# Sums of squares of the DeltaNet queries: from transposes and ScalarE squares to products with a column of ones

## The chip, the cores and the metric

The kernel runs on one NeuronCore of one Trainium2 chip. The metric is the device time of one execution in microseconds (us), as the median of several executions of the same program. Profiles are taken of one execution each. The five engines are named as in the profile: PE (TensorE matmul; PEld is its weight load), DVE (VectorE), ACT (ScalarE), POOL (GpSimd) and SP (SyncE, which issues most of the DMAs).

## The reference, cut to what matters

The kernel computes a two-layer encoder trunk over 1024 tokens of width 1024. The first (even) layer has mLSTM heads and gated DeltaNet heads that share one input projection; the second has a convolution and dilated attention. The part that the change touches is the normalisation of the DeltaNet queries, one of four heads of 128 channels at a time:

```python
def _l2n(t):
    return t * lax.rsqrt(jnp.sum(t * t, axis=-1, keepdims=True) + EPS)
...
    qkv = jax.nn.silu(_dwconv(dqkv, dn_conv_w))
    bq, bk, bv = _split(qkv, (B_HEADS * B_DK, B_HEADS * B_DK, B_HEADS * B_DV))
    q = _l2n(bq.reshape(bsz, s, B_HEADS, B_DK).astype(f32)) * (B_DK ** -0.5)
    k = _l2n(bk.reshape(bsz, s, B_HEADS, B_DK).astype(f32))
```

Each query is divided by the root of the sum of its 128 squares. The kernel leaves the queries as they are and brings the factor in at the end, on the output of the heads (`rq2` and `rqs`, from `ssq`). So for each head a number per token is needed, the sum over channels of the squared query, and it is needed only late.

## The kernel before, in words

**Layout.** Projections come out of PE as channels by tokens: 128 channels of one head on the partitions, 1024 tokens in the row, in two halves of 512 tokens. A projection (`project`, `prod`) is 24 matmuls of 128x512 for each half (three products of split operands for each of 8 blocks of the width). The halves go to two PSUM banks (`ibank`, two buffers), and a half can start only when the bank that it takes has been copied out.

**A query head, `dn_q(h)`.** ScalarE copies both halves into a page `xp` with a margin for the convolution (line 397). `conv5` makes the five taps on VectorE from `xp` into a page `y` (lines 402 and 404), then ScalarE writes the tanh into `xp` (line 405) and VectorE multiplies it back into `y` (line 406), which finishes the SiLU up to a factor of two. `y` is stored to HBM (`qT_d`, line 731). Then, for each half of the tokens, `turn` transposes four blocks of 128x128 with PE into a PSUM bank of the tag "t", and `squares` reads each block with a ScalarE Square whose accumulator gives the sum over the row (line 411): tokens stand on the partitions there, so the sum over channels is a sum along the row. Each such Square is followed by an instruction that reads the accumulator into a column of `ssq`. The key heads (`dn_k`) do the same, but need the transposed keys anyway.

**What the heads share.** Pages with the tag "b" (128x1024 float32) have three buffers, and every head takes two of them, one for `xp` and one for `y`; the mLSTM values take one each. A page is taken again when all readers of its last tile are done. The PSUM tag "t" has one buffer: the turns of keys, gate rows, queries, values and mLSTM keys and values all pass through it one after the other, and so do the products of the modulation (`ada_cols`, and `gps` in `modulation`).

**Order.** The steps are called in a fixed list: `dn_q` of head 0, `dn_v` of head 0, `m_q` 0, `dn_q` 1, `m_q` 1, then `systems`, `dn_q` 2 and 3, `m_k` 1, `m_v` 0, 2, 3, 1, `m_k` 0, and then the inversion of the DeltaNet systems, the mLSTM and the rest. From `systems` on, each half of a projection that ends issues one `dn_system` behind its last matmul on PE (`pace["sys"]`): products of keys (`KK`), decays on POOL and ScalarE, products on VectorE (line 649) and stores to `nd_d`, which the inversion reads when all eight are there. A generator, `modulation`, is stepped at each weight load and puts its loads, ScalarE scalings (line 444), POOL sums (line 446) and products between. Within these bounds a planner in the compiler orders each engine's instructions by its own simulated time and assigns the buffers; engines then run their instructions in that order.

`adaps` in the trace is a bank that holds products of the same kind as those of the change: 128 columns of weights against the column `one` (line 139 is the line of every matmul, line 158 that of every transpose).

Of the kernel before, what the change touches and what calls it, by code (L numbers as in the profile page):

```python
# [11 lines left out]
AF = mybir.ActivationFunctionType  # L12
# [5 lines left out]
P = 128  # L18
T = 1024
D = 1024  # L20
KT = 8
NCH = 8
# [34 lines left out]
def trunk(ctx, tc, x, c, norm_g, ada_w, ada_b, ev_w_in, ev_m_gate_b, ev_dn_dt_bias, ev_dn_a_log,  # L57
          ev_dn_conv_w, ev_m_norm_g, ev_dn_norm_g, ev_w_out, od_w_in, od_dw_w, od_dw_b, od_ln_g,
          od_ln_b, od_w_out, rel_bias, final_g, sel, onehot, seen, out):
    nc = tc.nc  # L60
# [40 lines left out]
    def page(name, shape=(P, T), dt=F32, tag="b"):  # L101
        return pg.tile(list(shape), dt, tag=tag, name=name, bufs=PAGES[tag])
# [3 lines left out]
    def bank(name, shape=(P, 512), tag="t"):  # L106
        return psb.tile(list(shape), F32, tag=tag, name=name, bufs=BANKS[tag])
# [19 lines left out]
    def nm(s):  # L127
        uid[0] += 1
        return f"{s}_{uid[0]}"
# [7 lines left out]
    def mm(o, l, r, s, e, shared=False):  # L137

        return nc.tensor.matmul(o, lhsT=l, rhs=r, start=s, stop=e, skip_group_check=shared).ins  # L139
# [3 lines left out]
    one = cst.tile([P, 1], F32, name="one")  # L143
# [12 lines left out]
    def tr(o, i):  # L156
        k = i.shape[0]
        nc.tensor.transpose(o, i, ident[:k, :k])  # L158
# [128 lines left out]
    def in0(c0, name, use):  # L287
        project(wsplit(w0[:, c0:c0 + P], name), hT, name, use)
# [26 lines left out]
    def columns(g):  # L315
        for tiles, b0 in zip(ada[g], (2 * g, 8 + 2 * g)):
# [5 lines left out]
                          in_=wgr.rearrange("p k (g c) -> p k g c", g=4))  # L322
# [67 lines left out]
    ssq = cst.tile([P, NCH, 4], F32, name="ssq")  # L390
    ivr = cst.tile([P, NCH, 4], F32, name="ivr")

    def conv_in():
        xp = page(nm("xp"), (P, T + 4))
        nc.gpsimd.memset(xp[:, 0:2], 0.0)
        nc.gpsimd.memset(xp[:, T + 2:T + 4], 0.0)
        return xp, lambda hf, ps: nc.scalar.copy(out=xp[:, 2 + hf * 512:514 + hf * 512], in_=ps)

    def conv5(xp, cidx, y):

        w_ = lambda j: cw[:, j * 12 + cidx:j * 12 + cidx + 1]
        nc.vector.tensor_scalar(out=y, in0=xp[:, 0:T], scalar1=w_(0), scalar2=None, op0=ALU.mult)
        for j in range(1, 5):
            nc.vector.scalar_tensor_tensor(out=y, in0=xp[:, j:j + T], scalar=w_(j), in1=y, op0=ALU.mult, op1=ALU.add)
        nc.scalar.activation(out=xp[:, 0:T], in_=y, func=AF.Tanh, scale=0.5)
        nc.vector.scalar_tensor_tensor(out=y, in0=xp[:, 0:T], scalar=1.0, in1=y, op0=ALU.add, op1=ALU.mult)

    def squares(b_, ss, q, h):
        junk = wk.tile([P, P], F32, tag="junk", name=nm("junk"))
        for i in range(4):  # L410
            nc.scalar.activation(out=junk, in_=b_[:, i * P:(i + 1) * P], func=AF.Square,
                                 accum_out=ss[:, q * 4 + i, h:h + 1])

    def turn(src, q, tag="t"):
        b_ = bank(nm("turn"), tag=tag)
        for i in range(4):
            tr(b_[:, i * P:(i + 1) * P], src[:, (q * 4 + i) * P:(q * 4 + i + 1) * P])
        return b_
# [54 lines left out]
    for h in range(2):  # L473
        xp, use = conv_in()
# [6 lines left out]
    for h in range(2, 4):  # L481
        xp, use = conv_in()
# [86 lines left out]
    for e in range(2):  # L569
        nc.sync.dma_start(out=woldb[e * 64:e * 64 + 64],  # L570
                          in_=wold_d.rearrange("(d q e) c -> e d q c", d=2, e=2)[e:e + 1].to_broadcast([64, 2, 2, NCH]))
# [6 lines left out]
    for src, dst in ((cs1, col1), (cs2, col2)):  # L578
        for q in range(2):
            b_ = turn(src, q)  # L580
            nc.vector.tensor_copy(out=dst[:, q * 4:q * 4 + 4, :].rearrange("p c (g r) -> p c g r", r=8),
                                  in_=b_.rearrange("p (c g r) -> p c g r", c=4, g=4)[:, :, :, 0:8])
# [143 lines left out]
    def dn_q(h):  # L726
        xp, use = conv_in()
        in0(1552 + h * P, "dq", use)
        y = page(nm("qT"))
        conv5(xp, h, y)  # L730
        nc.sync.dma_start(out=qT_d[h], in_=y)
        for q in range(2):
            squares(turn(y, q), ssq, q, h)

    def dn_v(h):
        xp, use = conv_in()
# [190 lines left out]
    for step, n in [(dn_q, 0), (dn_v, 0), (m_q, 0), (dn_q, 1), (m_q, 1), (systems, 0), (dn_q, 2), (dn_q, 3), (m_k, 1), (m_v, 0), (m_v, 2), (m_v, 3), (m_v, 1), (m_k, 0)] + [(dn_inverse, 0), (mlstm, 0), (dn_v, 1), (gate_chunk, 0), (dn_v, 2), (gate_chunk, 1), (dn_v, 3)]:  # L927
        step(n)
# [264 lines left out]
    for g, (a0, n) in enumerate(((0, N1), (N1, N23))):  # L1193
        for h in range(8):
            nc.sync.dma_start(out=z_d[g, h].rearrange("(q l) -> q l", l=513)[:, 0:n],
                              in_=nb_d[h:h + 1, a0:a0 + n].to_broadcast([P, n]))
# [411 lines left out]
```

## Time and profile before

| | |
|---|---|
| median of 3 runs | 1437.38 us (1429.26 to 1439.33) |
| the profiled execution | 1441.71 us, its span 1439.9 us |
| granted PE clock, mean of the span | 0.951 |
| PE busy | 1319.2 us (92%), 7299 instructions |
| DVE busy | 881.4 us (61%) |
| ACT busy | 589.2 us (41%), 1411 instructions |
| POOL busy | 471.8 us (33%) |
| largest shares of the chain that ended last | PE 59%, DVE 15%, DMA 15%, ACT 4% |

The span is the time from the first to the last instruction of the profiled execution. Busy time is the sum over an engine's instructions, where overlapping ones count once. PE's clock has two levels, 1.2 and 2.4 GHz; a granted clock of 0.50 is the lower one throughout and 1.00 the upper one. The chain that ended last is followed back from the last instruction, at each step to what released it.

### The profile page before, as it was taken

What the parts mean: (1) busy time and instruction counts of PE and PEld (TensorE: products, weight loads), DVE (VectorE), ACT (ScalarE), POOL (GpSimd) and SP (SyncE); (2) the same over time, 40 slices, a digit from 0 to 9 for tenths busy, and PEclk for the clock granted to TensorE, in tenths of its full rate; (3) what the DMA queues carried; (4) which work ended last, traced back from release to release, by engine and by line L of the source; (5) the groups of instructions that cost most, each with busy time, mean ns of one, the idle gap of its engine ahead of it and who ended that gap; (6) DMA issues with size and microseconds to landing.
All of it is one profiled execution on the core that took longest, in us unless ns stands there. A gap on an engine that the chain in (4) does not pass through costs nothing.

```text
span 1439.9 us, 20401 instructions
## 1 busy us (share of the span) xinstructions
PE 1319.2 (92%) x7299; PEld 1049.9 (73%) x7299; DVE 881.4 (61%) x1622; ACT 589.2 (41%) x1411; POOL 471.8 (33%) x357
## 2 busy tenths in 40 slices
PE   3887989988989999999999978999999999998998
PEld 2776767866777777888788757767777777776776
DVE  6779647169445332558654469997895553436444
ACT  5354575444645225544543211132326634335222
POOL 3455546443534412103340124211243232123120
PEclk9898889999999999899999989999999999998999
DMA  9433446746997786656651632111241153335412
GB/s 311 133 88 112 120 132 199 170 121 183 320 210 224 238 234 190 187 155 196 210 187 42 152 81 59 45 30 41 91 124 32 54 175 95 108 122 182 125 62 103
DMA packets 232985, 203.02 MB, mean 141 GB/s; under 512 B 59360, under 2 KB 191092, under 8 KB 232756
## 3 DMA queue, kind: packets, MB, share of 16 engines
q1 hardware_dynamic: 212083, 191.23, 45.1%
q10 hardware_dynamic: 20800, 10.49, 2.5%
q8 instruction: 58, 0.95, 0.3%
q14 instruction: 44, 0.35, 0.1%
HBM read 148.45 MB, written 56.88 MB: 143 GB/s over the span
## 4 chain that ended last, share of the span: by engine, by line
PE 59%; DVE 15%; DMA 15%; ACT 4%; SPq 3%; issue 3%; POOL 2%; POOLq 0%; ACTq 0%; DVEq 0%
PE y L139 12%; PE z L139 8%; PE sc L139 4%; DVE u L1247 4%; PE ob L139 3%; PE gb L139 3%; PE dq L139 2%; PE av L139 2%; PE pT L158 2%; PE ak L139 2%; PE mo L139 2%; PE mq L139 2%; PE aq L139 2%; PE ga L139 2%; DVE U L212 1%
## 5 line engine op out<-in xcount | busy, mean ns | idle before, releaser
L265 POOL TENSOR_TENSOR wlo<-wraw,whi 128x1024 fp32r<-128x1024 f32 x60 | 162.0, 2702 | 344.3 <-ACT whi L264 344.3
L1247 DVE SCALAR_TENSOR_TENSOR u<-xp,U,u 128x1009 f32<-128x1009 f32 (+14 forms) x120 | 175.0, 1491 | 1.0
L264 ACT CAST whi<-wraw 128x1024 fp32r<-128x1024 f32 x60 | 62.7, 1046 | 131.0 <-PE gb L139 46.3
L446 POOL TENSOR_TENSOR U<-U 128x512 f32<-128x512 f32 x56 | 81.9, 1463 | 75.7 <-ACT U L444 74.8
L139 PE MATMUL z<-hhi,wlo 128*128 128x512 f32 x256 | 104.5, 408 | 0.0
L139 PE MATMUL z<-hhi,whi 128*128 128x512 f32 x256 | 104.2, 407 | 0.0
L139 PE MATMUL z<-hlo,whi 128*128 128x512 f32 x256 | 103.9, 406 | 0.0
L139 PE MATMUL y<-wohi,mhi 128*128 128x512 f32 x240 | 97.4, 407 | 2.6 <-ACT mhi L1056 2.1
L139 PE MATMUL y<-wolo,mhi 128*128 128x512 f32 x240 | 96.5, 402 | 0.2 <-POOL wolo L1048 0.2
L139 PE MATMUL y<-wohi,mlo 128*128 128x512 f32 x240 | 95.9, 401 | 0.1
L444 ACT ACTIVATE U<-U,cs 128x512 f32<-128x512 f32 x64 | 46.1, 723 | 66.6 <-DMA U<-in_ada_w_dram 64.2
L1399 DVE COPY U<-pT 128x512 f32<-128x512 f32 x48 | 32.5, 688 | 52.7 <-PE pT L158 52.5
L602 POOL TENSOR_SCALAR_AFFINE_SELECT E<-E 128x512 f32<-128x512 f32 x32 | 23.7, 743 | 107.4 <-DMA E<-gc_d 59.0
L139 PEld LDWEIGHTS z<-hlo,whi 128*128 128x128 f32 x256 | 48.7, 190 | 12.3 <-issue 2.0
L139 PEld LDWEIGHTS z<-hhi,wlo 128*128 128x128 f32 x256 | 48.7, 190 | 11.5 <-issue 0.8
L139 PEld LDWEIGHTS z<-hhi,whi 128*128 128x128 f32 x256 | 48.8, 190 | 11.3 <-issue 0.7
L139 PEld LDWEIGHTS y<-wohi,mhi 128*128 128x128 f32 x240 | 45.8, 192 | 13.4 <-ACT mhi L1056 2.5
L139 PEld LDWEIGHTS y<-wohi,mlo 128*128 128x128 f32 x240 | 45.6, 190 | 11.5 <-DVE mlo L1057 0.9
L139 PEld LDWEIGHTS y<-wolo,mhi 128*128 128x128 f32 x240 | 46.0, 192 | 10.7 <-POOL wolo L1048 0.4
L1376 ACT ACTIVATE pt<-pt,o 128x256 f32<-128x256 f32 (+1 forms) x64 | 31.3, 489 | 53.3 <-DVE o L1372 45.4
L1372 DVE CUSTOM_DVE_ANT_0 pt<-sc,U 128x256 f32<-128x256 f32 (+1 forms) x64 | 25.8, 403 | 40.0 <-PE sc L139 20.6
L139 PE MATMUL sc<-ak,aq 128*128 128x256 f32 (+1 forms) x128 | 44.4, 428 | 6.4 <-DVE o L1374 5.4
(453 smaller groups left out, 3584.6 us busy)
## 6 DMA issues: line engine op xcount, KB each, us to landing
wraw<-in_ev_w_in_dram SPq DMA_DIRECT2D x32, 512.0 KB
U<-in_ada_w_dram SPq DMA_DIRECT2D x64, 256.0 KB
wraw<-in_od_w_in_dram ACTq DMA_DIRECT2D x20, 512.0 KB
x<-in_x_dram SPq DMA_DIRECT2D x11, 512.0 KB
ada<-in_ada_w_dram SPq DMA_DIRECT2D x10, 512.0 KB
od_d<-o SPq DMA_DIRECT2D x64, 66.0 KB
U<-od_d SPq DMA_DIRECT2D x4, 1056.0 KB
U<-gc_d SPq DMA_DIRECT2D x8, 512.0 KB
```

The source lines that it names most:

```text
L139: return nc.tensor.matmul(o, lhsT=l, rhs=r, start=s, stop=e, skip_group_check=shared).ins
L158: nc.tensor.transpose(o, i, ident[:k, :k])
L212: nc.vector.scalar_tensor_tensor(out=acc, in0=w_, scalar=cs[:, k:k + 1], in1=acc, op0=ALU.mult, op1=ALU.add)
L264: nc.scalar.copy(out=hi, in_=raw)
L265: nc.gpsimd.tensor_tensor(out=lo, in0=raw, in1=f(hi), op=ALU.subtract)
L444: nc.scalar.mul(out=t_ if k else acc, in_=t_, mul=cs[:, k:k + 1])
L446: nc.gpsimd.tensor_tensor(out=acc, in0=acc, in1=t_, op=ALU.add)
L602: nc.gpsimd.affine_select(out=ap, in_=ap, pattern=[[0, 4], [pat, P]], compare_op=ALU.is_ge, fill=NEG, base=0, channel_multiplier=cm_)
L1247: nc.vector.scalar_tensor_tensor(out=y[:, lo:hi], in0=xp[:, lo + d:hi + d], scalar=w_, in1=y[:, lo:hi], op0=ALU.mult, op1=ALU.add)
L1372: nc.vector.tensor_tensor_reduce(out=x1_, in0=ps[:, c0:c1], in1=bias[:, e, c0:c1], scale=1.0, scalar=1e30, op0=ALU.add, op1=ALU.min, accum ...
L1376: nc.scalar.activation(out=x1_, in_=x1_, func=AF.Exp, scale=-1.0, bias=mn1, accum_out=o2[:, 0, 128 + e:129 + e])
L1399: nc.vector.tensor_copy(out=PT, in_=tb)
```

## The change

For each of the four query heads, ScalarE squares the whole of `y` once, as channels by tokens, into the page `xp`. Eight products then take a block of 128 channels by 128 tokens of the squares as weights and the column of ones as the moving operand: each gives the sums over channels of 128 tokens as one column, tokens on the partitions, in one bank of the tag "t". VectorE copies the eight columns to `ssq`. The eight transposes of the head, its eight ScalarE squares by token and the eight reads of the accumulator go. `y` is then read last by the Square and the store, and `xp` by the products.

```diff
@@ -729,8 +729,12 @@
         y = page(nm("qT"))
         conv5(xp, h, y)
         nc.sync.dma_start(out=qT_d[h], in_=y)
-        for q in range(2):
-            squares(turn(y, q), ssq, q, h)
+
+        nc.scalar.activation(out=xp[:, 0:T], in_=y, func=AF.Square)
+        ps = bank(nm("sq"), (P, NCH))
+        for ch in range(NCH):
+            mm(ps[:, ch:ch + 1], xp[:, ch * P:(ch + 1) * P], one, True, True)
+        nc.vector.tensor_copy(out=ssq[:, :, h:h + 1], in_=ps.rearrange("p (c o) -> p c o", o=1))
```

## Rows read from the trace of the kernel before

**Rows 1.** The page, busy time: us, share of the span, instructions.

```profile
PE 1319.2 (92%) x7299; PEld 1049.9 (73%) x7299; DVE 881.4 (61%) x1622; ACT 589.2 (41%) x1411; POOL 471.8 (33%) x357
```

**Rows 2.** Busy by stretch: stretch, us, engines' busy us, granted clock, DMA share, GB/s.

```profile
195.00:235.00 40.00, 31.89 (x129) 23.80 (x128) 27.32 (x48) 24.23 (x76) 22.25 (x18) 0.79 0.67 190
```

**Rows 3.** Timeline of PE, 199 to 231 us: start, us, instruction [idle before <-releaser].

```profile
199.91 0.60 PE L158 MATMUL turn<-ident,qT 128*128 128x128 f32 x4
202.17 0.66 PE L158 MATMUL turn<-ident,qT 128*128 128x128 f32 x4 [1.21 <-ACT junk L411]
204.48 1.86 PE L139 MATMUL gps<-U,one 128*1 128x512 f32 x2 [1.66 <-ACT junk L411]
...
210.80 0.79 PE L139 MATMUL dq<-hhi,whi 128*128 128x512 f32 x1 [0.68 <-ACT xp L397]
...
228.25 1.12 PE L158 MATMUL turn<-ident,qT 128*128 128x128 f32 x4 [2.08 <-ACT junk L411]
230.29 0.79 PE L139 MATMUL mk<-hhi,whi 128*128 128x512 f32 x1 [0.93 <-ACT xp L397]
```

**Rows 4.** Instructions of `junk`: ns min/median/max, first and last start.

```profile
L411 ACT ACTIVATE junk<-turn x64: 244/277/300, 114.8 to 269.2; 128x128 f32<-128x128 f32 x64
L411 ACT ACTIVATION_READ_ACCUMULATOR junk<-turn x64: 185/194/229, 115.0 to 269.3; 128x1 f32 x64
...
L229 ACT ACTIVATE junk<-x x8: 1044/1057/1064, 4.3 to 38.1; 128x1024 f32<-128x1024 f32 x8
```

**Rows 5.** Instructions of `turn`, those on the queries.

```profile
L158 PE MATMUL turn<-ident,qT x32: 270/272/476, 199.9 to 267.7; 128*128 128x128 f32 x32
```

**Rows 6.** Instructions of `adaps`.

```profile
L139 PE MATMUL adaps<-one,U x64: 164/250/373, 13.5 to 418.1; 128*128 128x1 f32 x64
L220 DVE TENSOR_TENSOR modc<-adaps,vec x12: 140/151/162, 14.8 to 418.3; 128x2 f32<-128x2 f32 x8, 128x4 f32<-128x4 f32 x4
```

**Rows 7.** Timeline of PE around four products with the column of ones.

```profile
273.38 0.40 PE L139 MATMUL mv<-hhi,whi 128*128 128x512 f32 x1
273.62 0.95 PE L139 MATMUL adaps<-one,U 128*128 128x1 f32 x8
274.43 0.48 PE L139 MATMUL mv<-hlo,whi 128*128 128x512 f32 x1
274.75 0.40 PE L139 MATMUL mv<-hhi,wlo 128*128 128x512 f32 x1
```

**Rows 8.** Chain that ended last, in order of time: start, us, what.

```profile
148.31 7.78 PE mq L139 x23
...
164.21 7.04 PE dq L139 x30
...
200.07 0.44 PE turn L158 x4
...
203.44 4.64 DMA nd_d<-U
```

**Rows 9.** Timeline of DVE: last step of query head 0, value head 0, query head 1.

```profile
157.71 1.21 DVE L406 SCALAR_TENSOR_TENSOR qT<-xp,qT 128x1024 f32<-128x1024 f32 x1
159.02 0.75 DVE L402 TENSOR_SCALAR vT<-xp,cw 128x1024 f32<-128x1024 f32 x1
...
166.75 1.23 DVE L406 SCALAR_TENSOR_TENSOR vT<-xp,vT 128x1024 f32<-128x1024 f32 x1 [1.19 <-ACT xp L405]
...
217.87 1.23 DVE L406 SCALAR_TENSOR_TENSOR qT<-xp,qT 128x1024 f32<-128x1024 f32 x1 [5.62 <-ACT xp L405]
```

**Rows 10.** Timeline of ACT: copies of query heads 1 and 3 into their pages.

```profile
168.53 0.60 ACT L397 COPY xp<-dq 128x512 f32<-128x512 f32 x1
...
229.66 1.06 ACT L397 COPY xp<-dq 128x512 f32<-128x512 f32 x2
```

**Rows 11.** Timeline of SP: the store of query head 0.

```profile
162.33 0.55 SPq L731 DMA_DIRECT2D qT_d<-qT  x1
```

**Rows 12.** Timeline of PE: the first matmul behind the projection of query head 1.

```profile
174.33 0.39 PE L139 MATMUL mq<-hhi,whi 128*128 128x512 f32 x1
```

## The prediction

> **What bounds the kernel now.** I read the page's busy times first: PE is busy 92% of the span, no other engine over 61% [rows 1]. So a change pays where it takes away PE's idle time, its time at the low clock, or work on PE; time taken from ScalarE alone is hidden. Then I read busy time by stretch, where the query heads run. The stretch of 195 to 235 us is the poor one: PE is busy 31.89 of 40 us, so idle for 8.1, at a mean granted clock of 0.79 [rows 2]. The timeline of PE names the reason. The two turns of query head 0 stand one behind the other, since the one bank "t" must first be emptied by four ScalarE squares: 1.21 us of idle before the second turn, 1.66 before the next user of the bank. Head 1 has the same at 228.25, with 2.08 us [rows 3]. And twice PE starts a projection late, at 210.80 and 230.29, because ScalarE had not copied the last one out [rows 3]; that copy waited for a page "b", and the pages were held by tiles whose turns stood in the queue for the bank. So here bank "t" and the three pages set the pace together, and the change touches both: it shortens the stay in the bank and changes which page of a head is held to the end.
>
> **The change part by part.**
>
> *ScalarE.* 32 squares of 0.277 us and as many reads of 0.194 go, 15.1 us if none overlapped. Four squares of 128x1024 come, at 1.06 us each by the row of the same function on the same shape, 4.2 us [rows 4]. Some 11 us less for an engine at 41% [rows 1]: alone worth nothing, since PE hides it.
>
> *PE's work.* The 32 transposes that go [rows 5] cost 0.44 us for four [rows 8], 3.5 us in all. What comes is of the kind of the 64 rows of `adaps`, which stand for 32 products in the code, two rows to each [rows 6]. In the middle of a projection, four of them (eight rows) make the time from one matmul to the second one after it 274.75 - 273.38 = 1.37 us [rows 7]. Two steps of a projection at full clock take 2 x 7.04/30 = 0.47 us [rows 8]. So four products cost 0.90, a head's eight 1.8, all 32 cost 7.2 us. PE gets 3.7 us more work, 0.92 for each head. For heads 0 and 1 it falls into the idle time shown above; for heads 2 and 3 it lies between full projections, so 1.85 us are on the path.
>
> By the Trainium skill, page "TensorE: Matmul & The Clock Gate", section "Back-to-back issue gap", a matmul with 1 to 64 moving columns comes about every 25 ns at best, which is an estimate of 1.6 us for 64 rows; the row of this case says 0.11 us a piece, and the sum goes by the row.
>
> *VectorE.* Four copies of 128x8 out of PSUM. The nearest row is 0.151 us, a 128x2 or 128x4 read of such a bank [rows 6]: 0.6 us on an engine at 61%, nothing on the path. Each waits for the products, and what is queued behind it waits as well; the convolution of the next head could be caught there for the 1.8 us of the products.
>
> *Bank "t".* Head 0 holds it from 199.91 to 204.48, 4.6 us [rows 3]. Afterwards it is 1.8 for the products, 0.15 for the copy and two handovers, about 2.1. The gain of 2.5 us lets the users behind it go earlier, the value turns and with them the page for the next copy.
>
> *Pages, head 0.* This is the part that speaks against the change. Now `xp` of head 0 is free when line 406 ends, at 158.9, and the value head starts in it at 159.02 [rows 9]. After the change `xp` is held until the products, which stand behind the gate rows' turns in the bank, around 200 us. The page that comes free instead is that of `y`, when the Square (about 160) and the store are done. The store is issued at 162.33 [rows 11] and no row shows its landing; the nearest is a store of half the bytes, 4.64 us [rows 8]. I take that value: 167.0, with 162.9 (issue only) and 171.6 (twice the time for twice the bytes) as ends. The value head starts 8.0 us later (3.9 to 12.6). VectorE ends its line 406 at 168.0 now [rows 9], at 176.0 then (171.9 to 180.6). Only there is the page for query head 1 free: its first copy goes from 168.53 [rows 10] to 176.0 and ends at 176.6, and the matmul that takes that bank, at 174.33 now [rows 12], waits 2.3 us (0 to 6.9). A start at the low clock cost 7.78 - 23 x 0.235 = 2.4 us at 148.31 [rows 8]; I count it whole. Together 4.7 us (0 to 9.3), and all that follows on PE, the key systems included, moves by it.
>
> *Pages, head 1.* Head 1 ends line 406 at 219.1 [rows 9], so at 223.8 then. Square 1.06, products 1.8, a handover: `xp` is free at 226.8, and head 3 can be copied then and not at 229.66 [rows 10], because only one stay in the bank stands before it in place of two. The projection of `mk` starts 2.9 us earlier than its 230.29 [rows 3], with the 4.7 already in the count. What is late next is the second store and the second head's page; `y` of head 2 starts later, but only the sums wait for it, and the mLSTM values have another page by then.
>
> *Sum.* -2.9 + 1.85 = -1.0 us against the profiled execution's 1441.7 us (1.8 more than its span of 1439.9), so 1440.7. That execution stands 4.3 over the median of the runs shown, 1437.4; against that the forecast is **1436**. With the ends of the page term it lies between -5.7 (no stall) and +3.6, so 1431 to 1441.
>
> **The rivals.**
>
> *Slower: the pages.* The stall that I count once comes at each head that takes the place of one held by products: value head 0 and query head 1, then `y` of head 2, then `y` of head 3. Place: the page "b" behind each `xp`. Price: three times 4.7 and the 1.85, with no gain at head 1, +16 us: 1453. It decides when a head's products are placed later than the store's landing plus one convolution. For it: between 159 and 200 us all three pages are full, and a value head that started at once now starts with the store. Against it: from head 1 on, nothing but the products themselves is in the bank.
>
> *Faster: the whole poor stretch closes.* If the shorter stay lets the planner draw the bank's users together, 195 to 235 us lose their 8.1 us of idle. A mean clock of 0.79 with levels 0.5 and 1 means 0.42 x 40 = 16.8 us at the low one, at least 8.7 of them busy, so 4.35 us lost [rows 2]. 12.5 less 1.85: -10.6, 1427. For it: the gaps before turns name ScalarE's squares. Against it: the copy at 229.66 would wait for the convolution of head 1 anyway, which sat 5.62 us behind a tanh of ScalarE [rows 9].
>
> *The products cost twice as much.* If each took four passes and not the two rows seen, 32 would cost 14.4 us, and PE would have 10.9 us more work, 5.4 on the path in place of 1.85: 1440. The Trainium skill, page "FP8 and Floating Point Precision", section "TensorE Precision Notes", gives four passes for true fp32; here the trace shows two rows to a product and 0.11 us to a row, so it bears the rule out only if each row hides two. Little chance.
>
> *Nothing reaches the path.* The planner hides the stalls it makes and the gains: 1437.
>
> **How the numbers follow.** A measurement of this kernel can't tell less than about 1%, 14 us, from no change. Forecast 0.40, at 1436. Pages, slower: 0.23, at 1453, of which 0.19 beyond 1%. Poor stretch closes: 0.23, at 1427, of which 0.15 beyond 1%, since the planner lays out all engines anew and the systems that start earlier can add to it. Twice the price: 0.05. Nothing: 0.09. The time is that of the likeliest, 1436, whose own range is 1431 to 1441. The range that leaves out no more than 2 in 10 reaches well into both outer cases: 1420 to 1453. Faster by over 1%: 0.15; slower by over 1%: 0.19; within: 0.66.
>
> **What would show it.** In the profile after: `sq` with 64 matmul rows of some 0.11 us each between projections; no reads of the accumulator on queries; value head 0 starting some 8 us behind the end of line 406; PE waiting for the copy of query head 1; `mk` starting some 3 us before 230.29. The forecast is wrong if the first value head starts at once (then the page order is another than I think), if the stretch from 195 to 235 keeps its 8 us of idle, or if PE waits for copies at each head.

## The result, and the profile after

The changed kernel takes 1454.5 us, the median of 11 runs (1447.1 to 1458.8), where the kernel before took 1439.3 on the same chip (11 runs, 1429.3 to 1446.0). The ratio is 1.0108, with a 95% interval of 1.0085 to 1.0130: some 15 us slower. The forecast was 1436, no change, in a range up to 1453. The profiled execution took 1454.8 us with a span of 1453.0, 13.1 more than the span of before.

The busy times of the page, which answer to [rows 1]:

```profile
PE 1323.4 (91%) x7331; PEld 1056.5 (73%) x7331; DVE 884.2 (61%) x1626; ACT 584.3 (40%) x1351; POOL 472.7 (33%) x357
```

PE has 32 rows more and 4.2 us more of busy time, ScalarE 60 instructions less and 4.9 us less. So of the 13.1 us by which the span grew, 4.2 are busy time of PE, about what the products cost over the transposes, and 8.9 are idle time. The new operations, from the view of the tile `sq` (duration in ns as minimum/median/maximum, then first and last start):

```profile
L139 PE MATMUL sq<-one,xp x64: 164/250/271, 206.4 to 261.3; 128*128 128x1 f32 x64
L737 DVE COPY ssq<-sq x4: 154/168/173, 208.3 to 261.6; 128x8 f32<-128x8 f32 x4
```

There are 64 rows for 32 products, two to a product, and the timeline below gives a head's sixteen 1.84 us. The stretches that answer to [rows 2] (columns as there: PE, PEld, DVE, ACT, POOL busy, then the clock, the DMA share, GB/s), with the 45 us ahead of them:

```profile
150.00:195.00 45.00, 40.24 (x170) 32.11 (x169) 21.21 (x26) 21.72 (x62) 19.64 (x15) 0.90 0.37 101
...
195.00:235.00 40.00, 33.74 (x164) 27.21 (x164) 25.40 (x44) 24.60 (x63) 19.44 (x18) 0.87 0.56 167
```

The poor stretch got a little better: 33.74 us busy at a clock of 0.87 in place of 31.89 at 0.79. But the stretch ahead of it, in which PE was busy for all 45 us before, now has 4.8 us of idle. DVE's timeline of the same time answers to [rows 9]:

```profile
157.35 1.21 DVE L406 SCALAR_TENSOR_TENSOR qT<-xp,qT 128x1024 f32<-128x1024 f32 x1
168.11 0.75 DVE L402 TENSOR_SCALAR vT<-xp,cw 128x1024 f32<-128x1024 f32 x1 [9.56 <-DMA qT_d<-qT]
...
175.91 2.10 DVE L406 SCALAR_TENSOR_TENSOR vT<-xp,vT 128x1024 f32<-128x1024 f32 x1 [1.18 <-ACT xp L405]
...
205.15 0.22 DVE L622 TENSOR_TENSOR ckef<-cc,kef 128x64 f32<-128x64 f32 x1 [2.52 <-ACT kef L597]
208.28 0.17 DVE L737 COPY ssq<-sq 128x8 f32<-128x8 f32 x1 [2.90 <-PE sq L139]
208.36 1.62 DVE L402 TENSOR_SCALAR qT<-xp,cw 128x1024 f32<-128x1024 f32 x1
209.90 1.63 DVE L649 SCALAR_TENSOR_TENSOR U<-KK,ncc,U 128x128 f32<-128x128 f32 x6
211.45 1.92 DVE L404 SCALAR_TENSOR_TENSOR qT<-xp,cw,qT 128x1024 f32<-128x1024 f32 x1
213.30 0.59 DVE L649 SCALAR_TENSOR_TENSOR U<-KK,ncc,U 128x128 f32<-128x128 f32 x2
213.82 0.67 DVE L459 TENSOR_TENSOR grow<-gps,grow 1x512 f32<-1x512 f32 x1
```

Value head 0 starts at 168.11, when the store of the queries has landed, and not right behind line 406. Further on DVE stands idle for 2.90 us ahead of the copy of the sums (line 737), with the convolution of query head 1 behind it in the queue, which starts at 208.36 where it started at 203.07 before. The chain that ended last names the store as the piece between (start, duration, what):

```profile
161.71 6.28 DMA qT_d<-qT
168.11 0.77 DVE vT L402
```

PE's timeline, to be held against [rows 3] and [rows 12]:

```profile
178.76 0.79 PE L139 MATMUL mq<-hhi,whi 128*128 128x512 f32 x1 [4.76 <-ACT xp L397]
...
206.40 1.84 PE L139 MATMUL sq<-one,xp 128*128 128x1 f32 x16
...
208.72 1.02 PE L139 MATMUL gps<-U,one 128*1 128x512 f32 x2
...
214.54 1.11 PE L158 MATMUL turn<-ident,vT 128*128 128x128 f32 x4 [4.80 <-DVE grow L459]
...
218.23 0.80 PE L139 MATMUL dq<-hhi,whi 128*128 128x512 f32 x1 [0.68 <-ACT xp L397]
...
236.83 0.47 PE L139 MATMUL mk<-hhi,whi 128*128 128x512 f32 x1
```

The same turn of the values in the kernel before:

```profile
207.11 1.11 PE L158 MATMUL turn<-ident,vT 128*128 128x128 f32 x4 [0.77 <-DVE grow L459]
```

Three things are to be seen. `mq` waits 4.76 us in the middle, where it waited for nothing at 174.33. The 1.66 us of idle ahead of `gps` and the 2.08 at 228 us are gone, as the shorter stay in the bank promised. And in their place the turn of the values waits 4.80 us, where it waited 0.77: the bank is still held by `gps`, whose reader (`grow`, line 459) stands in DVE's queue behind two taps of the convolution of query head 1 and eight operations of the key systems, all of them let go together at 208.3. So the projection of head 3 starts at 218.23 and not at 210.80, and `mk` at 236.83 and not at 230.29.

The front is not all of it. The product `y` closes both layers; the first of it, at the end of the even layer, starts at 712.3 and not at 702.3, so 10.0 us late. The first step of the odd layer's query projection and the last steps of the final product, of the kernel before and then of the changed one, from the views of the tiles `aq` and `y` (first and last start):

```profile
L139 PE MATMUL aq<-hhi,whi x64: 387/396/496, 916.5 to 1264.0; 128*128 128x512 f32 x64
L139 PE MATMUL y<-wohi,m7hi x16: 390/392/398, 1387.7 to 1432.4; 128*128 128x512 f32 x16
```

```profile
L139 PE MATMUL aq<-hhi,whi x64: 387/395/500, 926.2 to 1274.7; 128*128 128x512 f32 x64
L139 PE MATMUL y<-wohi,m7hi x16: 390/391/392, 1400.8 to 1445.5; 128*128 128x512 f32 x16
```

From the first `aq` to the last `y`, a stretch whose code the change doesn't touch, the kernel before takes 515.9 us and the changed one 519.3. One mark between the two will be needed, the first transpose of values (`vps`) in the third of the odd layer's four turns of attention, on PE's timeline of the kernel before and of the changed one:

```profile
1193.31 0.27 PE L158 MATMUL vps<-ident,av 128*64 128x128 f32 x1
```

```profile
1205.69 0.27 PE L158 MATMUL vps<-ident,av 128*64 128x128 f32 x1
```

There the changed kernel is 12.4 us late, of 13.1 at the end. A single profile carries some microseconds of its own in this stretch, as the experiments show, so what it is worth has to come from several kernels.

### The profile page after: what moved, and what is told of

It is laid out like the page before. It is cut to its first block, busy times and chain, and to the rows that moved or that the text cites. A ratio compares the mean times of both kernels' runs of the same rounds, so it can differ in the third digit from the quotient of the medians.

```text
span 1453.0 us, 20433 instructions
## 1 busy us (share of the span) xinstructions
PE 1323.4 (91%) x7331; PEld 1056.5 (73%) x7331; DVE 884.2 (61%) x1626; ACT 584.3 (40%) x1351; POOL 472.7 (33%) x357
## 4 chain that ended last, share of the span: by engine, by line
PE 58%; DVE 17%; DMA 13%; ACT 5%; issue 3%; POOL 2%; SPq 2%; POOLq 0%; ACTq 0%; DVEq 0%
PE y L139 12%; PE z L139 9%; PE sc L139 4%; DVE u L1251 4%; PE gb L139 3%; DMA U<-in_ada_w_dram 3%; PE ob L139 3%; PE av L139 2%; PE pT L158 2%; PE ga L139 2%; PE mo L139 2%; PE ak L139 2%; PE dq L139 2%; DVE U L212 1%; DMA E<-nmu_d 1%
## 5 line engine op out<-in xcount | busy, mean ns | idle before, releaser
L139 PEld LDWEIGHTS z<-hlo,whi 128*128 128x128 f32 x256 | 48.2, 188 | 12.4 <-issue 2.2
```

## The experiments

Three theories went into them. *Page*: the page of head 0's queries, held until their store has landed, is the loss. *Work*: the products themselves are. *Planner*: the planner that orders each engine's instructions lays the later stages out otherwise, once something earlier is changed, and that order is slower. Ratios are to runs of the kernel before on the same chip.

**The page order without products.** The kernel before, in which ScalarE copies `y` to `xp` and the turns read that.

```diff
         nc.sync.dma_start(out=qT_d[h], in_=y)
+        nc.scalar.copy(out=xp[:, 0:T], in_=y)
         for q in range(2):
-            squares(turn(y, q), ssq, q, h)
+            squares(turn(xp, q), ssq, q, h)
```

> Each query head keeps its transposes and its squares by token, but they read a plain ScalarE copy of y in the page xp, so xp is held to the end and y is freed by the copy and the store, as in the changed kernel. Page theory (the cost of the change is that xp of head 0 is held until its turn in bank t, so that value head 0 starts only when the store of y has landed): value head 0's convolution starts about 9 us later than in the kernel before, PE waits about 5 us for the copy of query head 1, and the time is 10 to 20 us over the kernel before. Work theory (the cost is the products on PE and their place in its order): no products here, 4 us of copies on ScalarE, within 4 us of the kernel before. Planner theory (any edit of these heads lays the rest out anew and costs or gives some 10 us, whatever it is): no tie to where value head 0 starts.

Measured: 1.0074 (1.0047 to 1.0102). The stall is there in full with no product in the kernel, and the loss is what the page theory expected; the planner theory allows it too. DVE's timeline:

```profile
165.96 0.75 DVE L402 TENSOR_SCALAR vT<-xp,cw 128x1024 f32<-128x1024 f32 x1 [9.29 <-DMA qT_d<-qT]
```

And PE's:

```profile
176.61 0.79 PE L139 MATMUL mq<-hhi,whi 128*128 128x512 f32 x1 [4.69 <-ACT xp L397]
```

**The products without the page order.** The changed kernel, with the squares of each half in a small tile of its own, so that `xp` is free at once.

```diff
-        nc.scalar.activation(out=xp[:, 0:T], in_=y, func=AF.Square)
         ps = bank(nm("sq"), (P, NCH))
-        for ch in range(NCH):
-            mm(ps[:, ch:ch + 1], xp[:, ch * P:(ch + 1) * P], one, True, True)
+        for q in range(2):
+            s2 = htile("s2")
+            nc.scalar.activation(out=s2, in_=y[:, half(q)], func=AF.Square)
+            for i in range(4):
+                mm(ps[:, q * 4 + i:q * 4 + i + 1], s2[:, i * P:(i + 1) * P], one, True, True)
```

> The products stay, but the squares are written in two halves of 512 tokens to small tiles of another pool, so that xp is free when the convolution ends, as before, and y after the squares and the store. Page theory: value head 0 starts right behind query head 0 as in the kernel before, PE doesn't wait at 178 us, and the time is that of the kernel before or up to 8 us less. Work theory: the 15 us of the changed kernel stay, or at least the 4 us of more work on PE. Planner theory: somewhere within 10 us of the kernel before.

Measured: 1.0046 (1.0025 to 1.0067). DVE's timeline shows value head 0 taken up at once:

```profile
158.17 0.75 DVE L402 TENSOR_SCALAR vT<-xp,cw 128x1024 f32<-128x1024 f32 x1
```

PE has no wait inside `mq`, and `mk` starts at 225.7, 4.6 us earlier than before. Still the kernel is slower than before, where the page theory expected it no slower. The 4.6 us are given back by the first `y` (703.1, before 702.3). So the stall at head 0 is not all of the loss; the products' own 3.7 us may be part of what is left.

**Head 0 apart from the other heads**, both ways. First head 0 as before and heads 1 to 3 changed, then head 0 changed and heads 1 to 3 as before (the core of the second edit, against the changed kernel; the first has `h == 0`):

```diff
+        if h > 0:
+            for q in range(2):
+                squares(turn(y, q), ssq, q, h)
+            return
         nc.scalar.activation(out=xp[:, 0:T], in_=y, func=AF.Square)
         ...
```

> Head 0 as before (turns and squares by token), heads 1 to 3 as changed. Page theory: the stall belongs to head 0 alone, so the time is within 5 us of the kernel before. Repeated stalls (each head costs a third of it): 10 us over. Work theory: three quarters of the changed kernel's loss, 11 us over.

> Head 0 as changed, heads 1 to 3 as before. Page theory: the whole loss of the changed kernel, 12 to 18 us over the kernel before, with value head 0 waiting for the store. Repeated stalls: a third, 5 us. Work theory: a quarter, 4 us.

Measured: 1.0067 (1.0037 to 1.0097) with head 0 as before, and 1.0143 (1.0118 to 1.0168) with head 0 changed. In the second the stall stands as in the changed kernel, on DVE's timeline:

```profile
165.61 0.75 DVE L402 TENSOR_SCALAR vT<-xp,cw 128x1024 f32<-128x1024 f32 x1 [9.36 <-DMA qT_d<-qT]
```

and on PE's:

```profile
176.26 0.80 PE L139 MATMUL mq<-hhi,whi 128*128 128x512 f32 x1 [4.48 <-ACT xp L397]
```

In the first it is gone (value head 0 at 157.94), `mk` starts at 226.9, and 0.67% are lost all the same, twice what the page theory allowed; the first `y` comes at 710.7, 8.4 us late. With head 0 changed alone the loss is more than any of the theories gave. The heads are not additive either: 0.67% and 1.43% against 1.08% for all four.

**The order of steps changed with the products.** The changed kernel, with the first mLSTM query head listed ahead of value head 0.

```diff
-    for step, n in [(dn_q, 0), (dn_v, 0), (m_q, 0), (dn_q, 1), ...
+    for step, n in [(dn_q, 0), (m_q, 0), (dn_v, 0), (dn_q, 1), ...
```

> The changed kernel, with the first mLSTM query head (mq 0) listed ahead of the first DeltaNet value head in the written list of steps. The value head still waits for query head 0's store, but mq 0 can now fill that time on PE. The order from the key systems of the inversion to the end comes out the same as in the kernel before on every engine. Page theory (the wait for the page of head 0 is the loss): the 4.7 us wait inside mq is gone, only the 3.7 us of added PE work is left, ratio 1.000 to 1.003 to the kernel before. Planner theory (the re-laid order of the later stages is the loss): the late order is that of before, so again 1.000 to 1.003, but with first y product at 700 to 706 us and the last stretch (first gb to the last output product) as long as before's. Work theory (the products themselves are the loss): 1.008 to 1.010 as in the changed kernel.

Measured: 1.0027 (1.0004 to 1.0049). The ratio is as the page and the planner theory expected, but for another reason than the first of them gave. The wait was not gone, it was twice as long, as PE's timeline shows:

```profile
175.43 0.80 PE L139 MATMUL mq<-hhi,whi 128*128 128x512 f32 x1 [9.92 <-ACT xp L397]
```

First `y` came at 707.7, later than the 700 to 706 expected; the gain over the changed kernel is mostly behind that. The order of instructions is before's on every engine only from 650 us on; between 128 and 620 us it is another, so the expectation was wrong there. Its rows of `aq` and `y`:

```profile
L139 PE MATMUL aq<-hhi,whi x64: 387/396/496, 918.6 to 1265.5; 128*128 128x512 f32 x64
L139 PE MATMUL y<-wohi,m7hi x16: 390/392/398, 1385.4 to 1430.1; 128*128 128x512 f32 x16
```

They are 511.5 us apart, against 519.3 in the changed kernel.

**The same swap on the kernel before**, with no products. The edit is that of the last diff, word for word, on the other kernel.

> Control: the kernel before, with the same swap of steps (mq 0 ahead of value head 0) and nothing else; no products. If the swap by itself is worth nothing: ratio 0.997 to 1.003. If the swap by itself gains (PE gets a projection to fill the time in which VectorE convolves), 0.990 to 0.997, and the run of the changed kernel with the swap is to be read against this one. Planner theory: the order behind the systems is re-laid here too, and costs 0.5% (1.005) although no page is held longer.

Measured: 1.0068 (1.0047 to 1.0090). So the swap is no gain by itself; it costs 0.7% there. The planner theory had about that number, but in this profile the loss stands in the front, with PE waiting 6.14 us for a copy inside `mq` and this long ahead of a turn:

```profile
211.66 1.12 PE L158 MATMUL turn<-ident,qT 128*128 128x128 f32 x4 [10.04 <-ACT junk L411]
```

Here `mk` starts at 240.5, 10.2 us later than before, and the end comes 10.1 later.

**Half tiles at head 0 alone.** The second experiment's edit, with the squares of the other heads left in `xp`:

```diff
-        nc.scalar.activation(out=xp[:, 0:T], in_=y, func=AF.Square)
+        for q in range(2):
+            s2 = htile("s2") if h == 0 else xp[:, q * 512:q * 512 + 512]
+            nc.scalar.activation(out=s2, in_=y[:, half(q)], func=AF.Square)
         ...
```

> The changed kernel, but at head 0 alone the squares go in two halves into free half tiles and the products read those, so that head 0's xp is free at once for value head 0, as before the change; heads 1 to 3 keep their squares in xp. Page theory: no wait of VectorE for the store (value head 0 starts at 158 us, not 168), no wait inside mq, ratio 1.000 to 1.003. Planner theory: the stall is gone from the trace, but the order behind it is laid anew and 4 to 8 us go there: ratio 1.003 to 1.006. Work theory: 1.008 to 1.010.

Measured: 1.0093 (1.0061 to 1.0126). Value head 0 starts at 156.64 and `mk` at 227.4, 9.4 us earlier than in the changed kernel, and the time is that of the changed kernel. The first `y` is 6.2 us late all the same (708.5). This is the end of the page theory as the one cause. The number is the work theory's, but half tiles at all four heads carry the same products and lose half as much.

**Work added and nothing held.** The kernel before, with eight products of the identity and a copy that nothing reads, at head 0:

```diff
         for q in range(2):
             squares(turn(y, q), ssq, q, h)
+        if h == 0:
+            ps = bank(nm("sq"), (P, NCH))
+            for ch in range(NCH):
+                mm(ps[:, ch:ch + 1], ident, one, True, True)
+            nc.vector.tensor_copy(out=extra[:, :, h:h + 1], in_=ps.rearrange("p (c o) -> p c o", o=1))
```

> Control: the kernel before with its turns and squares, and at head 0 also eight products of the identity with the column of ones into a bank and one copy out of it (a result that nothing reads). No page is held longer; PE gets 1.8 us more work. Page theory: 1.000 to 1.002. Planner theory: adding work at this place is enough to lay the later stages anew, ratio 1.003 to 1.007, lost behind 310 us. Work theory: one head's products cost a quarter of the 15 us, 1.003, lost before 235 us.

Measured: 1.0072 (1.0049 to 1.0095). `mk` starts at 230.9, as before, and the first `y` at 700.1, 2.2 us earlier than before. All of the loss in this profile is behind that, as the rows of `aq` and `y` show:

```profile
L139 PE MATMUL aq<-hhi,whi x64: 387/396/628, 913.1 to 1272.2; 128*128 128x512 f32 x64
L139 PE MATMUL y<-wohi,m7hi x16: 387/392/500, 1396.1 to 1436.2; 128*128 128x512 f32 x16
```

They are 523.1 us apart, 7.2 more than before. So eight products that hold no page cost 0.72% in the median of twelve runs, some ten microseconds, where they themselves take 3.58 us on PE (at a granted clock of 0.50; a head of the changed kernel takes 1.84 at 1.00). The profile does not locate the ten. Its execution is only 3.8 us longer than that of before, and 3.6 of them are there at the third `vps` (1196.9 for 1193.3), though all engines run in before's order from 270 us up to it.

**The hold made shorter, and made longer.** Two edits of the changed kernel at head 0. In the first most of the store is filled from tiles of the input, so that `y` is only held for 64 columns; in the second `y` is stored twice. The first keeps the changed kernel's order on every engine from 100 us on. With the second the order was to come out as before's from the key systems on; in the trace it is before's on every engine from 650 us on, and another between 160 and 620 us.

```diff
+        if h == 0:
+            nc.sync.dma_start(out=qT_d[h][:, 0:64], in_=y[:, 0:64])
+            nc.sync.dma_start(out=qT_d[h][:, 64:512], in_=f(hT[0][0][0])[:, 64:512])
+            nc.sync.dma_start(out=qT_d[h][:, 512:1024], in_=f(hT[1][0][0]))
+        else:
+            nc.sync.dma_start(out=qT_d[h], in_=y)
```

```diff
         nc.sync.dma_start(out=qT_d[h], in_=y)
+        if h == 0:
+            nc.sync.dma_start(out=dr.tile([P, T], F32, name="again"), in_=y)
```

> The changed kernel, but at head 0 only the first 64 of the 1024 columns are stored from y; the other columns of that store are filled from tiles of the input that are held anyway, so as many bytes move, but y is free when the short store has landed. The queries of head 0 are wrong. The order of instructions is that of the changed kernel on every engine. Page theory: value head 0 starts at 163 to 165 us in place of 168, mq waits 0 to 2 us in place of 4.8, first mk 3 to 5 us earlier than 236.8, and the time falls by most of the loss: ratio 1.000 to 1.004. Planner theory: the front moves by 3 to 5 us, but the later order is that of the changed kernel, so a good part of the loss stays: ratio 1.005 to 1.009. Work theory: 1.008 to 1.010.

> The changed kernel, with a second store of the whole y at head 0 (into a scratch tensor that nothing reads): the page of head 0 is held for two landings, but the order of instructions from the key systems to the end comes out as in the kernel before on every engine. Page theory: value head 0 starts 3 to 6 us later than 168, mq waits 7 to 11 us, and the time is worse than that of the changed kernel: ratio 1.012 to 1.016. Planner theory: the longer stall is in the trace, but the later order is before's: ratio 1.003 to 1.008, better than the changed kernel although the page is held longer.

Measured: 1.0076 (1.0056 to 1.0095) with the short hold and 1.0038 (1.0019 to 1.0057) with the long one. DVE's timeline with the short hold:

```profile
166.19 0.75 DVE L402 TENSOR_SCALAR vT<-xp,cw 128x1024 f32<-128x1024 f32 x1 [8.11 <-ACT junk L411]
```

PE's with the short hold:

```profile
176.86 0.79 PE L139 MATMUL mq<-hhi,whi 128*128 128x512 f32 x1 [3.05 <-ACT xp L397]
```

DVE's with the long hold:

```profile
169.09 0.75 DVE L402 TENSOR_SCALAR vT<-xp,cw 128x1024 f32<-128x1024 f32 x1 [10.74 <-DMA again<-qT]
```

PE's with the long hold:

```profile
178.86 0.80 PE L139 MATMUL mq<-hhi,whi 128*128 128x512 f32 x1 [5.04 <-ACT xp L397]
```

Both moved the hold by less than expected: the short one by 1.9 us, where the row now names squares on ScalarE as what ended last, and the long one by 1.0. The first is a small gain against the changed kernel that the intervals do not quite tell apart. The kernel with the longer wait is the faster one, by more than the intervals leave open between it and the changed kernel (1.0057 against 1.0085). So the hold does not set the size of the loss. What made this kernel faster is not settled by it alone, since its order differs from the changed kernel's between 185 and 620 us as well as late. Its rows of `aq` and `y`:

```profile
L139 PE MATMUL aq<-hhi,whi x64: 387/397/628, 925.0 to 1275.7; 128*128 128x512 f32 x64
L139 PE MATMUL y<-wohi,m7hi x16: 390/392/398, 1395.0 to 1439.6; 128*128 128x512 f32 x16
```

It comes to the first `aq` 8.5 us later than before, as the changed kernel does (9.7), and needs 514.6 us from there. At the third `vps` the two are level (1205.1 and 1205.7); behind it this kernel needs 234.5 us and the changed one 239.8.

**The second store on the kernel before**, as a control, with the last diff on that kernel:

> Control for the second store: the kernel before, with head 0's queries stored twice (the second time into a scratch tensor). Its page is held by the turns until 200 us anyway and the order of instructions is before's on every engine. Page, planner and work theory alike: 0.998 to 1.002. If the second store itself disturbs the loads of that stretch: 1.002 to 1.005, and e10 is to be read less that.

Measured: 0.9979 (0.9960 to 0.9998), 508.8 us from first `aq` to last `y`. (The expectation's e10 is the long hold.) The store costs nothing. Its instructions run in before's order, so 7.1 us between its profile and before's in that stretch (508.8 and 515.9) are what two executions differ by.

**All runs in one table.** The order was read from PE's timelines from 900 us on, with repeats of a tile drawn together, against that of the kernel before, and likewise where other engines or earlier stretches are spoken of; `vps` is the mark named above; the clock is the granted one, averaged over the timed runs of each.

| kernel | ratio | order from 900 us on | first `aq`, us | `aq` to last `y`, us | third `vps`, us | `vps` to last `y`, us | mean clock |
|---|---|---|---|---|---|---|---|
| before | 1 | (itself) | 916.5 | 515.9 | 1193.3 | 239.0 | 0.957 |
| before, two stores | 0.9979 | before's | 915.5 | 508.8 | 1188.8 | 235.5 | 0.959 |
| changed, steps swapped | 1.0027 | before's | 918.6 | 511.5 | 1193.4 | 236.7 | 0.955 |
| changed, long hold | 1.0038 | before's | 925.0 | 514.6 | 1205.1 | 234.5 | 0.955 |
| head 0 as before | 1.0067 | before's | 925.7 | 513.5 | 1205.1 | 234.1 | 0.955 |
| half tiles, all heads | 1.0046 | another, from 1207 us | 914.4 | 521.3 | 1197.5 | 238.2 | 0.956 |
| before, steps swapped | 1.0068 | another, from 1207 us | 922.7 | 519.7 | 1203.9 | 238.5 | 0.950 |
| before, work added | 1.0072 | another, from 1207 us | 913.1 | 523.1 | 1196.9 | 239.2 | 0.951 |
| page order alone | 1.0074 | another, from 1207 us | 919.3 | 515.9 | 1194.1 | 241.1 | 0.955 |
| changed, short hold | 1.0076 | another, from 1207 us | 918.3 | 520.4 | 1202.8 | 235.9 | 0.957 |
| half tiles, head 0 | 1.0093 | another, from 1337 us | 918.8 | 522.9 | 1200.4 | 241.3 | 0.953 |
| changed | 1.0108 | another, from 1207 us | 926.2 | 519.3 | 1205.7 | 239.8 | 0.951 |
| head 0 changed alone | 1.0143 | another, from 1207 us | 923.2 | 524.7 | 1207.2 | 240.7 | 0.948 |

Five profiles with before's late order need 508.8 to 515.9 us from the first `aq` on, 512.9 on the mean; eight with another order 515.9 to 524.7, 520.9 on the mean. But these 8 us are not the price of the late order. Up to the third `vps` all thirteen kernels run in one order on PE, DVE, ScalarE and POOL, and 4.7 of the 8 us lie there: 276.9 us on the mean of the five, 281.6 of the eight. Two things move that part. One is where a wait of PE falls. In each kernel one operation of POOL near the first `aq` (a `wlo`, the low part of split weights) takes 8.4 to 10.0 us, where the median of its kind is 2.4, and PE waits 3.4 to 4.9 us for it. In four kernels, before and the changed one among them, that is ahead of the first `aq`, in the other nine behind it. The changed kernel and then the long hold:

```profile
902.08 0.80 PE L139 MATMUL gb<-hhi,wlo 128*128 128x512 f32 x1 [4.27 <-POOL wlo L265]
```

```profile
930.53 0.79 PE L139 MATMUL aq<-hhi,wlo 128*128 128x512 f32 x1 [4.92 <-POOL wlo L265]
```

The other is the clock, granted at 0.95 to 0.99 from the first `aq` to the third `vps`.

Behind the third `vps`, where the orders part, the five need 236.0 us on the mean (234.1 to 239.0) and the eight 239.3 (235.9 to 241.3). PE is idle there for 3.7 to 6.0 us in the five and for 5.9 to 7.8 in the eight. So the late order is worth some 3 us, with ranges that overlap; in the profiles of before and of the changed kernel it is 0.7 us of 13.1.

The ratios go the same way without saying which stage it is. The three changed kernels with before's late order lose 0.27, 0.38 and 0.67%, or 4, 5 and 10 us of 1438; the changed kernel loses 15. But all three also run another order than the changed kernel between 240 and 600 us, and the products' own 3.7 us may be in each. The front is no measure of the page alone: the first `y` comes at 712.3 in the changed kernel, at 710.7 with head 0 as before and at 708.5 with half tiles at head 0, though these two have no stall.

## Why the prediction was wrong

**Sized right.** The products: 1.84 us a head, forecast 1.8. The Trainium skill, page "TensorE: Matmul & The Clock Gate", section "Back-to-back issue gap", would have made it, as an estimate, 1.6 us at best for all four heads; here they take 7.5, and the row of `adaps` was the one to go by. The Trainium skill's page "FP8 and Floating Point Precision", section "TensorE Precision Notes", gives four passes for true fp32; the trace shows sixteen rows to eight products, two each, as before. The copies: 0.17 us, forecast 0.15. ScalarE's relief was worth nothing, as said; its busy time fell by 4.9 us and not by the 11 of the instructions' sum, in part because each read of the accumulator overlapped its square.

**Pages, head 0: right mechanism, short by 2 us.** Value head 0 started at 168.1 (forecast 167.0) and behind the store. The store landed 6.28 us after its issue and not 4.64, issued a little earlier; line 406 took 2.10 us in place of 1.23; so `mq` waited 4.76 and not 2.3. Its last step moved from 185.7 to 192.2, 6.5 us, where 4.7 stood in the sum, within its ends of 0 and 9.3.

**Bank "t", and Pages, head 1: the gains that did not come.** This is the first step that failed, and the larger one. The forecast let the users behind the products go 2.5 us earlier, and `mk` start 2.9 us before 230.29. It started 6.5 us behind it, so 9.4 us of the 14.1 between forecast (1440.7 for the profiled execution) and measurement (1454.8) are there. The products did leave the bank earlier: `gps` came 4.2 us late where they had come 6.5 late. But the next user after `gps` waits for an addition on DVE, and the forecast went by who holds the bank and not by where in its queue the one stands who frees it. The text itself had named the place: the copy of the sums waits on DVE for the products, and the convolution of head 1 behind it. It was costed at nothing, with 1.8 us as its worst. It was 2.90 us, and it let two taps of the convolution, eight operations of the key systems and `grow` go in one run, so that PE waited 4.80 us for the bank in place of 0.77. The turn of the values was 7.4 us late, and the full 6.5 us of the first stall came through to `mk`. Nor did `mk` wait for the page of head 1, by which it was forecast for 227.4: that page was free when head 1's products ended at 230.95, and PE was busy with the projection of query head 3 until 234.6. In the kernel before that projection ends at 224.9, so by the forecast's own shifts (4.7 us, less 2.5 at the bank) it would have ended between 227.1 and 229.6, with the products of head 1 still to come, which left no room for 227.4.

**The sum: it ended at 235 us.** This is the second failure. The forecast let all later work move with `mk`, but for 1.85 us of products. The changed kernel takes 3.4 us more from `mk` to the first `y`, in another order of instructions, and 3.1 more from there to the end. The sentence that the planner lays out all engines anew stood in the rival of a gain, as an argument for its size, and was given no price on the other side. That there is a price is shown by the kernel with work added, which loses 0.72% with under 4 us of work and the front as before; in which stage it is paid is not shown.

**The rivals.** "Slower: the pages" came to 1453, a microsecond and a half off, but not by its mechanism. It wanted a stall at each of three heads. There is one; at heads 2 and 3 PE waits for no copy. And an experiment with no such stall (half tiles at head 0) is as slow. A right number by luck, since the trace refutes the mechanism. "The whole poor stretch closes" holds in part, since the gaps before `gps` and at 228 us closed; but the idle time moved ahead of them. "Twice the price" is refuted by the 1.84 us. And the 1% that a measurement was said to need was too much: the interval here is 0.23% to either side.

**What stays open.** The cause of the whole 15 us is not shown. The changed kernel's stall and its wait at the bank are measured, but kernels without the stall lose from 0.46 to 0.93%, and every edit that changed the order of instructions made the kernel slower. So the planner theory is the one that no run refutes, though half tiles at head 0 lost more than the range it gave. It remains argued: which instructions cost it, in the query heads' stretch, between 235 and 620 us or behind 1193, is not settled, and the planner also assigns the buffers anew. PE's late order first differs at about 1207 us, where the kernel before turns attention outputs and then projects a gate while others have scores there. In three of the slow kernels a score then waits 2.6 to 2.7 us for DVE, but not in the changed one. Part of it may be the clock: at a mean of 0.951 the changed kernel spends 2 x 0.049 x 1454 = 142 us at the lower level, the kernel before at 0.957 some 124. Work that takes twice as long there makes up to 9 us of this. But the kernels with half tiles at all heads and with the short hold are slow at 0.956 and 0.957, so it isn't the clock alone. A kernel with all products, no hold and before's order throughout was not run; no version with the products beats the kernel before.

## What to carry to other kernels

When an edit frees a buffer earlier, follow the chain to the instruction that frees it for the next user after that, and look at what stands ahead of it in its engine's queue. Where a planner orders the instructions, an edit of two microseconds can lay out stages a millisecond away anew: try a change with an edit beside it that does no work of its own, or bring the old order back, before its cost is blamed on its own lines. A stall that is seen in the trace, at the right place, is not thereby the loss: lengthen it, and see whether the time follows. And a loss is located by marks between which the orders can be compared: a mark that one wait can fall on either side of, as the first `aq` here, puts microseconds into the wrong stage.

## What the hardware showed

A store of 512 KB from one page held that page for 6.28 us from its issue, at a DMA share of 0.43 from 162 to 168 us; with a second store behind it the page was free only 1.0 us later. Sixteen rows of one column, each with a weight load of its own, took 1.84 us at a granted clock of 1.00 and 3.58 at 0.50. One operation of POOL (a `wlo`) took 8.4 to 10.0 us once in every profile, where the median of its kind is 2.4. Two executions of the same order differ by up to 7 us over 510 (508.8 and 515.9), so a stage of a single profile says little below that, and the medians of many runs have to carry a difference of half a per cent.
